# A hybrid encoder trunk: the passes for the attention row maxima in the projection stage, and two kinds of store on ScalarE's queue

## The chip, the cores and the metric

One core of one Trainium2 chip runs the whole program as one launch. The metric is the device time of that core in microseconds, the median over several executions. The profiles are each of one execution.

## The reference

Two batches of 1024 tokens (a "prompt" and a "sample") go through the same two layers. Each layer is a norm, one wide projection into four token mixers and their gates, the mixers, and one projection back:

```python
def _trunk(x, p):
    for l in range(DEPTH):
        h = _rmsnorm(x, p['norm_g'][l])
        zz = h @ p['w_in'][l]
        zA, zB, zC, zD = ...
        oA = _rwkv_mixer(zA, ...)          # A: matrix state, 4 heads of 64, both directions
        oB = _global_attn_mixer(zB, ...)   # B: 4 query heads on 2 key heads, rotary, all 1024 keys
        oC = _rglru_mixer(zC, ...)         # C: gated linear recurrence
        oD = _window_attn_mixer(zD, ...)   # D: window of 128 to both sides, ALiBi, a sink logit
        o = jnp.concatenate([oA, oB, oC, oD], -1) @ p['w_out'][l]
        x = x + o
    return _rmsnorm(x, p['final_g'])
```

B and D are softmax attention: `p = exp(s - m)`, with `m` the maximum of a query's row of scores (in D also of the sink). Any `m` near the maximum gives the same quotient.

## The kernel before

A unit u is one batch in one layer: u = 0, 1 are the two batches in layer 0, u = 2, 3 in layer 1. The program is written in the order `F0 F1 B0 O0 F2 B1 O1 F3 B23 O23`: F is `front` (norm, projections, mixers A and C), B is `mixer_bd` (attention of both kinds), O is the projection back. A scheduler at build time then fixes the order of the instructions on every engine, and each engine runs its own list strictly in that order. So parts of the program overlap: the long serial mixer A of a unit (chunks of 64 tokens, many small products on quarters of TensorE's array) runs beside that unit's projections, and its rest beside whatever follows.

**Projections.** `proj` makes a block of 128 output columns for all 1024 tokens: weights come in two pieces on ScalarE's queue, ScalarE rounds them (`wh`), GpSimd forms the rest (`wl`), and TensorE does 48 products of 512 columns into two PSUM buffers `pj`. A unit has 17 blocks that go to DRAM as `zd` (`proj_store`: ScalarE copies PSUM to `m`, SyncE's queue stores it) and 8 gate blocks (`proj_gate`). `ropes` normalises and rotates queries and keys of B and writes them back to `zd`; it uses the three PSUM buffers `px` and the SBUF buffers `rp`.

**Attention.** A unit has four jobs (`JOBS`): two of kind D, two of kind B, each with two query heads r on one key head. `attn_prep` loads queries and keys from `zd`, each twice, into both halves of the 128 partitions, and splits them into a rounded part and a rest (`ka`, `kb`, `qa`, `qb`). `attn_max` computes the row maxima: for each of the 8 blocks of 128 queries a product of 128 rows by 512 keys (B: two halves of the keys; D: up to 384 keys, and a second product that adds the ALiBi bias), and a `tensor_reduce` on VectorE (L930 in B, L942 in D). `put_max` turns the maxima round on TensorE, negates them on ScalarE, loads them as a row, and copies this into row 64 of `qb`, so that the scores' second product subtracts them. `attn_main` then goes over blocks of 128 keys: scores of both heads into `px`, exponentials on ScalarE (L982), the products with the values (L99), and sums of the exponentials on VectorE and GpSimd in turn (L995). `mixer_bd` steps the maxima of the next job between the blocks of the running job; those of the first job come before its first block.

## Time and profile before

| | |
|---|---|
| median of 3 runs | 3402.02 us (3401.68 to 3405.71) |
| the profiled execution: its time, its span | 3410.22 us, 3408.1 us |
| TensorE busy | 3097.8 us (91%) |
| VectorE busy | 1909.3 us (56%) |
| ScalarE busy | 1280.9 us (38%) |
| GpSimd busy | 1157.5 us (34%) |

A product's end is modelled, so that products of a dense stream overlap in the records, and 91% does not mean that TensorE could take no more. What bounds a stage has to be read stage by stage.

### The profile page before, as it was taken

The page shows a single profiled execution, that of the slowest core. Times are in us where ns is not written, and L with a number is a line of the kernel's source. Part 1 is how long each engine was busy: PE and PEld are TensorE (multiplying, and loading weights), DVE is VectorE, ACT ScalarE, POOL GpSimd, SP SyncE. Part 2 cuts the span into 40 slices and gives each one's busy share as a digit, 9 for nine tenths or more (in the row PEclk, how much of TensorE's full clock was granted, in tenths as well). Part 3 has the DMA queues.
Part 4 walks back from the last instruction along what each step waited for, and adds up shares of the span by engine and source line. Part 5 has one row for each costly group of instructions (what it writes and reads, how often), then busy time and mean ns, then how long its engine had stood idle before and what let it go on. Part 6 is the DMA issues. An engine that isn't in the chain of part 4 may idle for free.

```text
span 3408.1 us, 68337 instructions
## 1 busy us (share of the span) xinstructions
PE 3097.8 (91%) x27826; PEld 2166.3 (64%) x27826; DVE 1909.3 (56%) x3849; ACT 1280.9 (38%) x2429; POOL 1157.5 (34%) x1008
## 2 busy tenths in 40 slices
PE   6999999999789798999978988989999889977997
PEld 5777767766445576776756546766776555543586
DVE  6245344154887627135667765335563687698523
ACT  5332223225544324224444433226323434464322
POOL 2234232232433233223332333332332333435443
PEclk8999999999789897999968997889999779988999
DMA  7333333233310434233331015333333221123453
GB/s 248 116 106 102 92 112 96 90 102 103 105 43 24 135 122 123 79 94 101 121 101 56 20 45 163 113 100 104 115 105 96 76 68 36 37 63 133 161 200 133
DMA packets 382276, 344.06 MB, mean 101 GB/s; under 512 B 125709, under 2 KB 264969, under 8 KB 381961
## 3 DMA queue, kind: packets, MB, share of 16 engines
q1 hardware_dynamic: 242568, 270.48, 24.8%
q10 hardware_dynamic: 139392, 69.22, 7.2%
q8 instruction: 218, 3.57, 0.4%
q14 instruction: 98, 0.79, 0.1%
HBM read 217.84 MB, written 121.63 MB: 100 GB/s over the span
## 4 chain that ended last, share of the span: by engine, by line
PE 62%; DVE 19%; DMA 8%; ACT 4%; issue 4%; SPq 1%; POOL 1%; ACTq 0%; POOLq 0%; DVEq 0%
PE pj L101 36%; PE pa L101 11%; PE px L101 7%; PE pj L99 4%; DMA tg<-og 2%; DVE bk L567 1%; PE ps L101 1%; DVE bk L569 1%; DVE mxb L930 1%; SPq L95 1%; DMA halo<-zd 1%; DVE ac L995 1%; DVE b L904 1%; DMA bk<-nd 1%; DMA nd<-nl 1%
## 5 line engine op out<-in xcount | busy, mean ns | idle before, releaser
L101 PE MATMUL pj<-h,wh 128*128 128x512 f32 x3200 | 1072.7, 413 | 29.8 <-ACT h L236 11.0
L101 PEld LDWEIGHTS pj<-h,wh 128*128 128x128 f32 x3200 | 598.7, 191 | 217.0 <-issue 37.6
L326 POOL TENSOR_TENSOR wl<-wr,wh 128x512 fp32r<-128x512 f32 x264 | 351.7, 1332 | 951.5 <-ACT wh L325 848.8
L101 PE MATMUL pj<-h,wl 128*128 128x512 f32 x1600 | 645.9, 407 | 0.7 <-POOL wl L326 0.7
L101 PE MATMUL px<-b,b 128*128 128x512 f32 (+6 forms) x1072 | 361.5, 430 | 29.7 <-DVE mxb L930 12.7
L995 POOL TENSOR_TENSOR ac<-e,ac 128x512 f32<-128x512 f32 (+3 forms) x192 | 228.1, 1195 | 471.8 <-ACT e L982 321.8
L101 PEld LDWEIGHTS pj<-h,wl 128*128 128x128 f32 x1600 | 305.2, 191 | 82.9 <-issue 14.5
L101 PE MATMUL pj<-oh,wh 128*128 128x512 f32 x1024 | 334.3, 405 | 13.6 <-ACT oh L236 10.7
L101 PEld LDWEIGHTS px<-b,b 128*128 128x128 f32 (+1 forms) x1072 | 198.1, 207 | 221.3 <-issue 134.0
L325 ACT CAST wh<-wr 128x512 fp32r<-128x512 f32 x264 | 163.4, 619 | 465.7 <-PE pj L101 460.2
L982 ACT ACTIVATE e<-px 128x512 f32<-128x512 f32 (+3 forms) x384 | 191.4, 516 | 252.5 <-PE px L101 247.0
L101 PEld LDWEIGHTS pj<-oh,wh 128*128 128x128 f32 x1024 | 192.1, 191 | 64.8 <-ACT oh L236 14.6
L99 PE MATMUL pj<-e,v 128*64 128x512 f32 (+3 forms) x768 | 194.3, 573 | 11.7 <-ACT e L982 10.9
L101 PE MATMUL pj<-oh,wl 128*128 128x512 f32 x512 | 202.3, 400 | 0.0
L101 PE MATMUL pa<-ar,bk 64*64 64x128 f32 (+2 forms) x2560 | 142.7, 303 | 42.7 <-ACT nl L520 24.6
L995 DVE TENSOR_TENSOR ac<-e,ac 128x512 f32<-128x512 f32 (+3 forms) x192 | 144.3, 755 | 57.9 <-ACT e L982 38.0
L101 PEld LDWEIGHTS pa<-ar,bk 64*64 64x64 f32 x2560 | 106.5, 148 | 86.2 <-issue 42.8
L930 DVE TENSOR_REDUCE mxb<-px 128x1 f32<-128x512 f32 x160 | 108.2, 682 | 30.6 <-PE px L101 30.1
L348 ACT ACTIVATE m<-pj 128x512 f32<-128x512 f32 x136 | 80.8, 594 | 116.3 <-PE pj L101 100.3
L1081 DVE TENSOR_TENSOR xo<-xo,pj 128x512 f32<-128x512 f32 x64 | 43.8, 685 | 125.3 <-PE pj L101 97.4
L911 POOL TENSOR_TENSOR b<-rw,b 64x512 fp32r<-64x512 f32 x64 | 90.6, 1425 | 66.8 <-ACT b L910 66.0
L101 PEld LDWEIGHTS pj<-oh,wl 128*128 128x128 f32 x512 | 98.3, 192 | 21.6 <-issue 1.4
(285 smaller groups left out, 5010.9 us busy)
## 6 DMA issues: line engine op xcount, KB each, us to landing
wr<-in_w_in_dram ACTq DMA_DIRECT2D x200, 256.0 KB
zd<-m SPq DMA_DIRECT2D x136, 256.0 KB
tg<-og SPq DMA_DIRECT2D x64, 512.0 KB
rw<-zd SPq DMA_DIRECT2D x192, 128.0 KB
og<-m SPq DMA_DIRECT2D x64, 256.0 KB
wr<-in_w_out_dram ACTq DMA_DIRECT2D x64, 256.0 KB
xo<-xd SPq DMA_DIRECT2D x64, 256.0 KB
halo<-zd SPq DMA_DIRECT2D x56, 256.5 KB
```

The source lines that it names most:

```text
L95: self.nc.sync.dma_start(out=out, in_=src)
L99: return self.nc.tensor.matmul(out=out, lhsT=lhsT, rhs=rhs, start=start, stop=stop, skip_group_check=True)
L101: self.nc.tensor.matmul(out=out, lhsT=lhsT, rhs=rhs, start=start, stop=stop)
L325: nc.scalar.copy(out=hi, in_=raw)
L326: nc.gpsimd.tensor_tensor(out=lo, in0=raw, in1=hi.bitcast(F32), op=ALU.subtract)
L348: self.nc.scalar.mul(out=m, in_=p, mul=scale)
L567: nc.vector.tensor_tensor(out=ww, in0=m[:, j, j + 1:16].unsqueeze(2).to_broadcast([128, k, j + 1]), in1=t[:, j:j + 1, 0:j + 1].to_broadcas ...
L911: (nc.gpsimd if PQ else nc.vector).tensor_tensor(out=c[0:64, s], in0=t[0:64], in1=a[0:64, s].bitcast(F32), op=ALU.subtract)
L930: nc.vector.tensor_reduce(out=mx[:, i, half:half + 1], in_=p, axis=AX.X, op=ALU.max)
L982: last = nc.scalar.activation(out=e[:, :n], in_=p[:, :n], func=AF.Exp)
L995: (nc.gpsimd if (x + r) % ADDM else nc.vector).tensor_tensor(out=acc[r][:, os], in0=es[r][:, :n], in1=acc[r][:, os], op=ALU.add)
L1081: nc.vector.tensor_tensor(out=xo, in0=xo, in1=p, op=ALU.add)
```

## The change

The row maxima leave the attention. A generator `attn_maxes` runs inside `front`: for each of the four jobs it loads the keys of the head once more into both halves of the partitions and the queries of both heads, rounds both on ScalarE (`mk`, `rp`), and multiplies rounded queries with rounded keys only, head 0 on partitions 0 to 63 and head 1 on 64 to 127, so that the two heads' products use different halves of TensorE's rows. The reductions on VectorE are as many and as large as before. The maxima are stored to a DRAM tensor `rows`, from which `attn_prep` loads them. Four steps of the generator are written after each block of B's projections (a step: one block of queries, both heads, and in B one half of the keys), five after each gate block, and what is left after the last gate. The blocks are now written in the order D, B, C, with a step of `ropes` after each block of B and C. The stores of projected blocks and of maxima are issued on ScalarE's queue. `rp` has three buffers instead of five.

```diff
-MAXF = 1
-MXP = 3
-MXD = 3
+MAXB, MAXD = 5, 4
-BUFS = {..., "rp": 5, "cs": 1, ...
+BUFS = {..., "rp": 3, "mk": 2, "cs": 1, ...
...
+    def store_a(self, out, src):
+        self.nc.scalar.dma_start(out=out, in_=src)
...
     def proj_store(self, pool, wsrc, c0, h, dst, first=False, scale=1.0):
         def cb(half, p):
             m = self.t(pool, "m2")
             self.nc.scalar.mul(out=m, in_=p, mul=scale)
-            self.load(dst[:, HT * half:HT * half + HT], m)
+            self.store_a(dst[:, HT * half:HT * half + HT], m)
...
-    def put_max(self, pool, mr, qb):
...
     def attn_prep(self, pool, J):
...
+                row = self.t(pool, "rw")[64:65]
+                self.load(row, J["rows"][r].rearrange("n q -> (n q)").unsqueeze(0)[:, s])
+                nc.scalar.copy(out=c[64:65, s], in_=row)
...
-    def attn_max(self, pool, J, L):
...
+    def attn_maxes(self, pool, zd, L, rows, es):
+        def high(tag, srcs):
+            t = self.t(pool, "rp")
+            for hs, src in srcs:
+                self.load(t[hs], src)
+            h = self.t(pool, tag).bitcast(F32R)
+            nc.scalar.copy(out=h, in_=t)
+            return h
+        for job, (z, g) in enumerate(JOBS):
+            hs = [slice(HT * half, HT * half + HT) for half in range(2)]
+            kh = [high("mk", [(q, zd[z + 2][64 * g:64 * g + 64, s]) for q in HS]) for s in hs]
...
+            for i in range(NT):
+                if i % 4 == 0:
+                    qh = high("rp", [(slice(0, 128), zd[z + g][:, hs[i // 4]])])
+                q = lambda r: qh[HS[r], 128 * (i % 4):128 * (i % 4) + 128]
+                if z == ZD:
...
+                    for r in range(2):
+                        self.mm(ps[r][:, :n], self.slope[2 * g + r], self.alibi[:, b0:b0 + n], start=False, skip=True)
+                    for r in range(2):
+                        nc.vector.tensor_reduce(out=mx[r][:, i:i + 1], in_=ps[r][:, :n], axis=AX.X, op=ALU.max)
+                    yield
+                else:
+                    for half in range(2):
+                        ps = [self.px() for _ in range(2)]
+                        for r in range(2):
+                            self.mm(ps[r], q(r), kh[half][HS[r]])
+                        for r in range(2):
+                            nc.vector.tensor_reduce(out=mx[r][:, i, half:half + 1], in_=ps[r], axis=AX.X, op=ALU.max)
+                        yield
...
+                self.store_a(rows[job, r], m)
...
     def mixer_bd(self, units):
...
-            for _ in self.attn_max(pool, jobs[0], jobs[0]["L"]):
-                pass
             for i in range(len(jobs)):
-                nxt, ahead = iter(()), 0
                 if i + 1 < len(jobs):
                     start(i + 1)
-                    nxt = self.attn_max(pool, jobs[i + 1], jobs[i + 1]["L"])
...
+                self.attn_main(pool, jobs[i])
...
     def front(u):
...
                 k.mixer_a(keep, zd, L, od[0:2])
-                for b in range(2):
-                    k.proj_store(pool, wi, C_OFF + 128 * b, h, zd[ZC + b])
-                for b in range(4):
-                    k.proj_store(pool, wi, B_OFF + 128 * b, h, zd[ZB + b])
-                rope = k.ropes(pool, zd, L)
+                maxes = k.attn_maxes(pool, zd, L, rows, es)
                 for b in range(4):
                     k.proj_store(pool, wi, D_OFF + 128 * b, h, zd[ZD + b], scale=0.125 if b < 2 else 1.0)
-                    next(rope, None)
+                rope = k.ropes(pool, zd, L)
+                for off, n, z in ((B_OFF, 4, ZB), (C_OFF, 2, ZC)):
+                    for b in range(n):
+                        k.proj_store(pool, wi, off + 128 * b, h, zd[z + b])
+                        next(rope, None)
+                        for _ in range(MAXD if z == ZB else 0):
+                            next(maxes, None)
                 k.mixer_c(zd, L, od[4:6])
             for i, off in ((2, B_OFF + 512), (6, D_OFF + 512), (4, C_OFF + 256), (0, A_OFF + 896)):
                 for b in range(2):
                     k.proj_gate(pool, wi, off + 128 * b, h, gd[i + b])
-                    next(rope, None)
+                    for _ in range(MAXB):
+                        next(maxes, None)
+            for _ in maxes:
+                pass
```

Three places of the instruction order that the scheduler made.

VectorE, where unit 0 ends: before, from the last gate (L359) on. `m`, `h` in L307 and L237 are the norm of unit 1, `kt` is mixer A.

```order
L359 SCALAR_TENSOR_TENSOR m_901_6282<-m_901_6282,pj_6220 128x512
L359 SCALAR_TENSOR_TENSOR m_902_6286<-m_902_6286,pj_6221 128x512
L647 TENSOR_TENSOR kt_378_2205<-kt_378_2205,pa_2668 128x512
L307 SCALAR_TENSOR_TENSOR m_910_6310<-m_910_6310,par_122,rp_6301 128x512
L647 TENSOR_TENSOR kt_380_2207<-kt_380_2207,pa_2669 128x512
L307 SCALAR_TENSOR_TENSOR m_913_6317<-m_913_6317,par_122,rp_6308 128x512
L307 SCALAR_TENSOR_TENSOR m_914_6322<-m_914_6322,par_122,rp_6301 128x512
L237 TENSOR_TENSOR h_6313<-m_910_6310,h_6312 128x512
```

VectorE after the change, some 30 instructions behind the last gate of unit 0. L953 is the reduction of B's maxima, L692 the addition in the 14 state steps of mixer A (L689 before).

```order
L953 TENSOR_REDUCE mx_983_6366<-px_6372 128x1
L953 TENSOR_REDUCE mx_984_6367<-px_6373 128x1
L692 TENSOR_TENSOR z_258_1258<-z_258_1258,ps_2836 128x128
L953 TENSOR_REDUCE mx_983_6366<-px_6378 128x1
L953 TENSOR_REDUCE mx_984_6367<-px_6379 128x1
L953 TENSOR_REDUCE mx_983_6366<-px_6384 128x1
L692 TENSOR_TENSOR z_258_1258<-z_258_1258,ps_2842 128x128
L953 TENSOR_REDUCE mx_984_6367<-px_6385 128x1
L953 TENSOR_REDUCE mx_983_6366<-px_6390 128x1
L953 TENSOR_REDUCE mx_984_6367<-px_6391 128x1
L692 TENSOR_TENSOR z_259_1259<-z_259_1259,ps_2848 128x128
L953 TENSOR_REDUCE mx_983_6366<-px_6466 128x1
```

Before, the norm of unit 1 follows the last gate at once. Now 54 of unit 0's reductions stand behind that gate, in threes between mixer A's instructions, and the first instruction of unit 1's norm comes after the last of them. On TensorE, too, the first projection of unit 1 comes after unit 0's last product for maxima. In the four units 54, 49, 52 and 49 reductions, 204 of 384, stand behind the last gate; in units 1, 2 and 3 attention or its preparation follows.

TensorE after the change, in unit 0's projections. `pa` is mixer A, `px<-mk,rp` the new product of scores, `px<-alibi` the bias, `pj` a projection; the stretch had only `pa` and `pj` before.

```order
L103 MATMUL pa_1832<-na_270_1309,nl_264_1271 64x128
L103 MATMUL pa_1833<-na_272_1311,nl_264_1271 64x128
L101 MATMUL px_5100<-mk_5078,rp_5089 128x384
L101 MATMUL px_5100<-alibi,slope_456 128x384
L101 MATMUL px_5107<-mk_5078,rp_5089 128x384
L101 MATMUL px_5108<-mk_5078,rp_5089 128x384
L101 MATMUL px_5107<-alibi,slope_455 128x384
L101 MATMUL px_5108<-alibi,slope_456 128x384
L103 MATMUL pj_5269<-h_307,wh_5302 128x512
L103 MATMUL pj_5269<-h_306,wl_5303 128x512
L103 MATMUL pj_5269<-h_320,wh_5302 128x512
```

With three buffers `px` the products come in threes: one head alone first, then a pair of both heads. Of 208 pairs 146 stand next to each other. The 180 reductions that stand ahead of the last gates have 212 products of scores (128 reductions of D, whose blocks 3 and 4 need two products each, and 52 of B) and 128 of bias, in 75 such runs.

SyncE's queue in unit 0's projections: before, `zd<-m` are the stores of projected blocks, `nd`, `halo` and `wa` loads and stores of mixer A.

```order
L95 DMA zd_89<-m_218_1092 128x512
L95 DMA zd_89<-m_219_1095 128x512
L95 DMA zd_89<-m_228_1160 128x512
L95 DMA zd_89<-m_229_1163 128x512
L95 DMA nd_1576<-nl_264_1271 128x8x64
L95 DMA zd_89<-m_641_4758 128x512
L95 DMA zd_89<-m_642_4761 128x512
L95 DMA zd_89<-m_651_4826 128x512
L95 DMA zd_89<-m_652_4829 128x512
L95 DMA halo_1512<-zd_89 128x513
L95 DMA wa_1510<-wa_1505 128x512
L95 DMA halo_1519<-zd_89 128x513
```

After, at the place of mixer A's first inverse (`nd`, `td`, `bk` are its round trips through DRAM; `rp<-zd` are loads of ropes and of the maxima).

```order
L93 DMA bd_1260<-tp_1238 128x512
L93 DMA td_1577<-bk_287_1396 128x256
L93 DMA bk_287_1396<-td_1577 128x16x16
L93 DMA rp_5038<-zd_89 128x512
L93 DMA rp_5075<-zd_89 64x512 x2
L93 DMA rp_5080<-zd_89 64x512 x2
L93 DMA rp_5087<-zd_89 128x512
L93 DMA zd_89<-rp_5038 128x512
L93 DMA rp_5193<-zd_89 128x512
L93 DMA rp_5230<-zd_89 128x512
L93 DMA zd_89<-rp_5193 128x512
```

No store of a projected block is left on this queue; the loads for the maxima stand there instead, 64-row loads for keys and 128-row loads for queries, six for a job.

## Rows read from the trace of the kernel before

**Rows 1.** The page's first line

```profile
span 3408.1 us, 68337 instructions
```

**Rows 2.** Windows by stage: projections of units 0 and 1, three attention stages

```profile
core 0: us, PE busy (x) PEld busy (x) DVE busy (x) ACT busy (x) POOL busy (x), PEclk, DMA share, GB/s
...
57.00:421.00 364.00, 356.89 (x3077) 272.36 (x3078) 151.70 (x360) 118.53 (x231) 110.22 (x107) 1.00 0.38 117
...
456.00:836.00 380.00, 368.10 (x3536) 277.99 (x3535) 152.10 (x347) 117.91 (x221) 107.72 (x91) 1.00 0.31 93
836.00:1158.00 322.00, 266.92 (x2612) 152.96 (x2612) 258.01 (x487) 152.89 (x304) 120.27 (x113) 0.85 0.24 71
...
1718.00:2058.00 340.00, 288.70 (x3046) 176.46 (x3035) 248.69 (x504) 140.50 (x301) 115.69 (x112) 0.83 0.22 63
...
2633.00:3191.00 558.00, 482.55 (x4589) 275.95 (x4581) 432.48 (x796) 261.48 (x516) 220.87 (x185) 0.88 0.22 66
```

**Rows 3.** Groups by line: the reductions of the row maxima

```profile
L930 DVE TENSOR_REDUCE mxb<-px 128x1 f32<-128x512 f32 x160 | 108.2, 682 | 30.6 <-PE px L101 30.1
...
L942 DVE TENSOR_REDUCE mxd<-px 128x1 f32<-128x384 f32 (+1 forms) x80 | 41.2, 525 | 15.5 <-PE px L101 15.4
```

**Rows 4.** Windows: two attention jobs of kind B, the later one without maxima

```profile
3087.00:3151.00 64.00, 50.46 (x175) 20.61 (x170) 58.16 (x79) 30.18 (x54) 34.52 (x23) 0.93 0.46 157
3151.00:3192.00 41.00, 40.06 (x137) 15.82 (x136) 19.94 (x24) 18.35 (x34) 19.95 (x14) 0.90 0.04 13
```

**Rows 5.** Timeline of TensorE in the last attention job

```profile
3177.16 1.21 PE L101 MATMUL px<-b,b 128*128 128x512 f32 x4
...
3179.31 1.21 PE L101 MATMUL px<-b,b 128*128 128x512 f32 x4
...
3181.46 1.21 PE L101 MATMUL px<-b,b 128*128 128x512 f32 x4
```

**Rows 6.** Windows: last gate of a unit to the first exponential

```profile
836.00:880.00 44.00, 25.38 (x229) 16.81 (x230) 38.86 (x66) 31.58 (x48) 20.75 (x13) 0.76 0.49 150
...
1718.00:1766.00 48.00, 29.89 (x193) 22.25 (x183) 39.42 (x95) 21.76 (x48) 20.20 (x21) 0.62 0.54 154
...
2633.00:2674.00 41.00, 29.38 (x469) 21.38 (x462) 33.68 (x88) 19.14 (x41) 15.40 (x14) 0.59 0.50 143
```

**Rows 7.** Windows of the mixer's 14 state steps (L689 alone)

```profile
444.00:487.00 43.00, 4.00 (x14) 0.92 0.27 87
...
2702.00:2735.00 33.00, 3.93 (x14) 0.84 0.23 73
```

**Rows 8.** Timeline of TensorE: 64-row products between projections

```profile
113.04 1.12 PE L101 MATMUL pa<-wa,up 64*128 64x512 f32 x2
114.09 0.73 PE L101 MATMUL pj<-h,wh 128*128 128x512 f32 x2
...
165.05 0.63 PE L101 MATMUL pj<-h,wh 128*128 128x512 f32 x2
165.52 0.40 PE L101 MATMUL pj<-h,wl 128*128 128x512 f32 x1
165.85 1.13 PE L101 MATMUL pa<-wa,up 64*128 64x512 f32 x4
166.91 0.50 PE L101 MATMUL pj<-h,wh 128*128 128x512 f32 x1
```

**Rows 9.** Who waited for the maxima of kind B (us, times)

```profile
  PEld px L101: 22.9, 24
  PE pj L101: 17.6, 13
```

**Rows 10.** The waits of SyncE's queue, and one of the mixer on its loads

```profile
SPq L95 <- ACT m L348: 593.2, 118, 15.1
...
SPq L95 <- ACT mt L864: 223.1, 17, 33.3
...
ACT bk L579 <- DMA bk<-td: 44.7, 14, 8.6
```

More of the change, by code (lines that the diff above doesn't have):

```diff
@@ L250, in x_first @@
         h = []
+        rows = self.t(hpool, "cs", (128, 2, HT)) if hpool else None
         for half in range(2):
@@ L258, in x_first @@
             self.rms_finish(ss, st[:, 4 * half:4 * half + 4])
-            rb = self.norm_rows(hpool, st, half, self.px) if hpool else None
+            rb = self.norm_rows(rows, st, half, self.px) if hpool else None
             for d in range(ND):
@@ L275, in x_first, with norm_rows @@
         return h
-    def norm_rows(self, pool, st, half, ps):
+    def norm_rows(self, rb, st, half, ps):
         pb = ps()
@@ L282, in norm_rows @@
             self.mm(pb[:, 128 * j:128 * j + 128], st[:, i:i + 1].to_broadcast([128, 128]), self.ident)
-        r = self.t(pool, "rp", (128, 516))[:, 0:HT]
-        self.nc.scalar.copy(out=r, in_=pb)
-        return r
+        self.nc.scalar.copy(out=rb[:, half], in_=pb)
+        return rb[:, half]
     def rms_finish(self, ss, st):
@@ L296, in norm @@
         nc = self.nc
-        rb = [self.norm_rows(pool, st, half, self.pj) for half in range(2)]
+        rb = self.t(pool, "cs", (128, 2, HT))
+        rb = [self.norm_rows(rb, st, half, self.pj) for half in range(2)]
         h = []
@@ L856, in diag @@
                                      in1=x.unsqueeze(2).to_broadcast([128, n, 128]), op=ALU.mult)
-    def put_max(self, pool, mr, qb):
-        nc = self.nc
-        p = (self.pj if PJ & 2 else self.px)((NT, 128))
-        nc.tensor.transpose(out=p, in_=mr.bitcast(F32), identity=self.ident)
-        m = self.t(self.smp, "mt", (NT, 128), bufs=1)
-        nc.scalar.mul(out=m, in_=p, mul=-1.0)
-        for half in range(2):
-            row = self.t(pool, "e")[64:65]
-            self.load(row, m[4 * half:4 * half + 4])
-            nc.scalar.copy(out=qb[64:65, HT * half:HT * half + HT], in_=row)
     def values(self, pool, src):
@@ L983, in attn_main @@
                     es.append(e)
-                    yield
                 for r in range(2):
@@ L1012, in mixer_bd @@
             jobs = []
-            for zd, L, od in units:
+            for zd, od, rows, es in units:
                 vals = {}
-                for z, g in JOBS:
+                for n, (z, g) in enumerate(JOBS):
                     jobs.append({"g": g, "q": zd[z + g], "k": zd[z + 2][64 * g:64 * g + 64], "alibi": z == ZD, "z": z,
-                                 "vals": vals, "vs": zd[z + 3], "L": L, "o": od[(6 if z == ZD else 2) + g]})
+                                 "vals": vals, "vs": zd[z + 3], "rows": rows[n], "es": es[g],
+                                 "o": od[(6 if z == ZD else 2) + g]})
             def start(i):
@@ L1027, in mixer_bd @@
             start(0)
-            for _ in self.attn_max(pool, jobs[0], jobs[0]["L"]):
-                pass
             for i in range(len(jobs)):
-                nxt, ahead = iter(()), 0
                 if i + 1 < len(jobs):
                     start(i + 1)
-                    nxt = self.attn_max(pool, jobs[i + 1], jobs[i + 1]["L"])
-                    ahead = (16 if jobs[i + 1]["alibi"] else 32) * MAXF / (20 if jobs[i]["alibi"] else 32)
-                due = 0
-                for _ in self.attn_main(pool, jobs[i]):
-                    due += ahead
-                    while due >= 1:
-                        next(nxt, None)
-                        due -= 1
-                for _ in nxt:
-                    pass
+                self.attn_main(pool, jobs[i])
     def space(self, st, name, pad=0):
@@ L1174, in front @@
         od, gd = [[og[d][:, i] for d in range(ND)] for i in range(2)]
-        zog.append((zd, od, og))
+        rows = k.t(k.drp, "mx", (len(JOBS), 2, NT, 128), bufs=2)
+        es = [[], []]
+        zog.append((zd, od, og, rows, es))
         wi = w["w_in"][l]
```

58 lines of the change are left out of this document (27 added, 31 removed).

## The prediction

> **What bounds the kernel now.** I read the page first, then the span cut into stages, then the places where a stage could be seen with and without the maxima. The stages follow each other almost without overlap except for mixer A, which runs beside all of them. The reader should see two kinds [rows 2]. In the projections (57 to 421 us, 456 to 836) TensorE is busy 357 of 364 and 368 of 380 us at a granted clock of 1.00, which is the level of 2.4 GHz, and VectorE only about 152 us. So there TensorE is the bound. In the three attention stages (322, 340 and 558 us, 1220 us together) VectorE is busy 258, 249 and 432 us, 939 us or 77%, and the granted clock is a mean of the two levels, 0.83 to 0.88: TensorE waits at times. The row maxima lie entirely in these stages: 256 reductions of kind B at 0.68 us and 128 of kind D at about 0.53 us [rows 3], 174 + 68 = 242 us, a quarter of VectorE's work there.
>
> What a maximum costs the attention can be read near the end, where mixer A is done. The last job but one of kind B runs with the 32 reductions of the last job between its blocks and takes 64 us; the last job has none beside it and takes 41 us [rows 4]. In the first VectorE is busy 58 of 64 us, in the second 20 of 41. In the second TensorE sets the pace: a block of keys starts every 2.15 us (3177.16, 3179.31, 3181.46) [rows 5].
>
> **The change part by part.** The sum is made against the profiled execution's span of 3408.1 us [rows 1] and its own time of 3410.2 us, which lies 8.2 us above the median of 3402.0.
>
> *Maxima out of the attention.* 64 - 41 = 23 us for 32 reductions is 0.72 us each, slightly more than the reduction itself. For 256 of kind B that gives 184 us; for 128 of kind D I take the bare 0.53 us, 68 us: **-252 us**. The other bound: beside mixer A VectorE is busy only 77%, and if only that share of the gain is real it is -194 us. I take the first, because the places with and without differ by nothing else as large.
>
> *The start of an attention stage.* From a unit's last gate to the first exponential 44, 48 and 41 us pass [rows 6], 133 us. In them the first job's 16 reductions, two heads' blocks of kind D, have to run alone, and then come the transposition, the load and the copy of the maxima. 16 x 0.53 = 8.5 us of each start are already counted. Of the remaining 107 us I take 25 us a start, **-75 us**: preparation can run beside what now precedes it, while the rest is mixer A's and C's work, which stays. Bounds: 0 and -107 us.
>
> *204 reductions behind the last gates.* The order shows them in threes, each three before one of mixer A's state steps where those run. Fourteen such steps take 43 us in one place and 33 us in another [rows 7], so 3.07 and 2.36 us a step, and three reductions and the addition are 3 x 0.68 + 0.28 = 2.32 us. So three reductions cost a step of 2.36 to 3.07 us, 0.79 to 1.02 each. I take 0.9: **+184 us**. The lower bound is the 0.72 of above, 147 us, the upper 1.02, 208 us. Nothing covers them: unit 1's norm is queued behind them on VectorE, and TensorE's first projection behind that; in the other units the attention is.
>
> *180 reductions beside projections.* VectorE has the room, but TensorE, the bound there, gets 212 products of scores and 128 of bias more. A projection's product of 512 columns goes by in 0.235 us (two start from 165.05 to 165.52) [rows 8]. At 352 columns a reduction of kind D needs 0.16 us for scores and 0.16 us for bias, one of kind B 0.235 us: 21 + 21 + 12 = 54 us if the heads do not overlap. They can: one 64-row product of 512 columns takes 1.05 us alone (113.04 to 114.09), and two on different halves of the rows take 1.06 us together (165.85 to 166.91) [rows 8]. If all pairs overlapped it would be 37 us; the order leaves 70% of the pairs next to each other, so 42 us. To enter the 64-row form costs 165.85 - 165.52 - 0.235 = 0.095 us [rows 8]; 75 runs make 7 us. Then TensorE waits for a free `px`: in the attention 256 reductions of kind B cost it 22.9 + 17.6 us of waits [rows 9], 0.16 us each, and for 180 that is 28 us. Together **+77 us**; bounds 37 us (all overlap, no waits) and 54 + 7 + 56 = 117 us (no overlap, twice the waits).
>
> The Trainium skill ("TensorEngine Tiling (Array Packing)", Key Properties) says that a change of tiling mode drains TensorE, which speaks against putting these runs between projections. The trace shows less: the last full product before the pair is recorded to 165.92, and the pair begins at 165.85, before it. By the rule each of the two changes of a run would cost the 0.165 us that a product outlasts its turn, 25 us in place of 7, and the time would come out 18 us later, inside the range below.
>
> *Queues and casts.* 136 stores of blocks and 32 of maxima pass from SyncE's queue to ScalarE's, and 64 more casts of about 0.6 us come to ScalarE. ScalarE is busy 118 us of 364 and 380 in the projections [rows 2], and this adds some 10 us of casts and 42 issues a unit; even at 0.5 us an issue it stays under half busy. I count nothing; if every issue held up an eviction of `pj` for 0.3 us it would be 50 us in all. On SyncE's queue the waits for projected blocks (593 us in total) and for maxima (223 us) go away [rows 10]. That is time in which the queue stood still, and loads behind it were late only if something wanted them; I count nothing here either and keep it as a rival. The new order of blocks D, B, C and the three `rp` buffers only shift work that is off TensorE's path; nothing.
>
> Sum: -252 - 75 + 184 + 77 = **-66 us**, so 3344 us for a profiled execution and **3336 us** as the median, 1.9% less.
>
> **The rivals.**
>
> 1. *Slower: the projections stall.* What was 0.16 us a reduction in the attention may be more beside projections, since VectorE runs mixer A, ropes and reductions in one strict order, and a run of three products needs all three `px` empty. If each of the 75 runs waits for three reductions, 2.04 us, the waits are 153 us instead of 28, and the sum is +59: 3461 us. It turns slower when a run waits more than 1.2 us. For it: TensorE has no slack there. Against it: the order puts some ten projections between runs, 2.4 us in which VectorE can empty two buffers.
>
> 2. *The reductions behind the gates eat it all.* If they come at 1.22 us each instead of 0.9, because unit 1's norm and the attention's preparation follow them one after another on VectorE, the sum is zero: about 3402 us. For it: VectorE's order has the whole norm behind them. Against it: in units 1 to 3 only preparation follows.
>
> 3. *More gain: SyncE's queue was the brake of mixer A.* ScalarE waits 44.7 us in total for one of the mixer's loads [rows 10], and the longest wait of the queue for maxima is 33.3 us, with the mixer's loads behind it. If those waits go and as much is saved on the mixer's other loads, some 90 us more are gained where mixer A runs beside attention: 3246 us.
>
> 4. *The packing changes nothing for TensorE*, because the pairs do not overlap in this form of product: 54 instead of 42 us, 12 us later. It stays inside the forecast.
>
> **How the numbers follow.** My forecast with rival 4 gets 0.52, rival 1 0.24, rival 2 0.11, rival 3 0.13. All the best bounds together (-252 - 107 + 147 + 37 = -175) would give 3227 us, all the worst (-194 + 0 + 208 + 117 = +131) 3533 us; neither is likely as a whole. The forecast's own range is 3270 to 3395 us. With rival 3 and the milder half of rival 1 the range that should hold the time 8 times in 10 is 3255 to 3440 us. A measurement of this kernel can tell about 0.2%, 7 us, from no change. Faster by more than that: nearly all of the forecast, rival 3 and a little of rival 2, 0.65. Within: 0.08. Slower: rival 1 and what is left of 2 and of the forecast, 0.27.
>
> **What the profile after would show.** Right: the attention stages of units 0 and 1 shrink from 322 and 340 us to some 200 to 240 us with TensorE the busiest and the clock nearer 1.00; between a unit's last gate and the next stage 50 to 90 us appear in which VectorE is nearly full of reductions and TensorE waits; each projection stage grows by 15 to 30 us. Wrong: a projection stage grows by more than 35 us with waits of `px` on the reductions (rival 1); the stretch behind a gate lasts over 100 us (rival 2); mixer A ends well before the last attention job and its waits on loads are halved (rival 3). The prediction is wrong, too, if attention keeps more than 280 us without its maxima, since then VectorE's time was not what it waited for.

## The result, and the profile after

The change makes the kernel slower: 3461.5 us (median of 4 runs) against 3403.9 us, 1.0148 times as long, 95% interval 1.0124 to 1.0173. A second comparison on another occasion gave 1.0145 (1.0117 to 1.0172). The prediction was 3336 us, faster, in a range that ends at 3440 us; it was wrong in sign.

The profiled execution took 3465.1 us. The page's first lines and its row of TensorE's granted clock:

```profile
span 3462.9 us, 68630 instructions
...
PE 3130.0 (90%) x27858; PEld 2195.0 (63%) x27858; DVE 1908.3 (55%) x3849; ACT 1312.5 (38%) x2493; POOL 1161.2 (34%) x1008
...
PEclk9999979999967889899997698899999958998998
```

The windows that answer to [rows 2]: projections of units 0 and 1, then the three stretches from a unit's last gate to the first product of the projection back (columns as there):

```profile
54.00:443.00 389.00, 376.15 (x3251) 287.79 (x3251) 174.61 (x416) 129.30 (x255) 111.17 (x107) 0.99 0.39 122
547.00:958.00 411.00, 393.33 (x3504) 292.51 (x3503) 179.20 (x406) 147.34 (x259) 113.06 (x97) 0.98 0.32 99
958.00:1264.00 306.00, 256.94 (x2651) 152.48 (x2651) 189.80 (x371) 123.09 (x259) 106.72 (x103) 0.77 0.22 65
1853.00:2167.00 314.00, 262.11 (x2810) 159.19 (x2804) 210.18 (x411) 129.48 (x273) 109.76 (x103) 0.78 0.23 64
2756.00:3247.00 491.00, 418.21 (x3793) 232.52 (x3791) 352.18 (x567) 250.28 (x482) 219.95 (x181) 0.84 0.25 76
```

The stretches from gate to projection back, 322, 340 and 558 us before, are still 306, 314 and 491 us, though VectorE's busy time in them has fallen by 68, 39 and 80 us. The granted clock fell too, from 0.85, 0.83 and 0.88. Their first 66, 70 and 53 us hold reductions that were moved here (below). The attention itself follows, with 240, 244 and 438 us:

```profile
1024.00:1264.00 240.00, 205.77 (x2053) 121.43 (x2047) 130.72 (x235) 106.81 (x223) 97.89 (x90) 0.83 0.21 64
1923.00:2167.00 244.00, 207.19 (x2512) 127.50 (x2512) 151.96 (x280) 112.97 (x236) 101.07 (x91) 0.84 0.22 66
2809.00:3247.00 438.00, 372.99 (x3271) 202.58 (x3271) 305.18 (x474) 242.12 (x462) 213.98 (x175) 0.86 0.26 79
```

Between units 0 and 1, where 35 us lay before, 104 us lie now (443 to 547); both figures include the first, sparse products of unit 1.

Where the time went is best seen in a table of places. Each number is the distance between starts of TensorE's products in the trace, in us: first to last product of a unit's projections, last gate to first product with the values, first to last product with the values, and so on. The columns are rounded one by one.

| kernel | four projection stages | unit 0's last gate to unit 1's first | last gates to values (3) | products with values (3) | values to projection back (3) | projection back (3) | rest | span |
|---|---|---|---|---|---|---|---|---|
| before | 1618 | 10 | 57+60+47 | 251+250+509 | 21+30+3 | 454 | 98 | 3408 |
| after | 1720 | 67 | 95+88+81 | 191+202+408 | 21+25+3 | 469 | 94 | 3463 |
| difference | +102 | +57 | +100 | -209 | -5 | +15 | -4 | +55 |

A second profile of the same changed kernel has 1728, 69, 264 and 791 us in the first four columns (1720, 67, 264 and 801 here). So a difference of 10 us in one column is no finding.

Behind the last gates the reductions of the global heads run. The four stretches from a last gate to the last reduction (two of them and the sum; the second fence counts L953 alone):

```profile
443.00:506.00 63.00, 55.43 (x641) 38.38 (x639) 52.70 (x123) 14.52 (x35) 6.27 (x5) 0.69 0.20 57
...
1853.00:1923.00 70.00, 54.92 (x298) 31.69 (x292) 58.21 (x132) 16.51 (x38) 8.70 (x12) 0.55 0.23 59
...
sum 251.00, PE 205.74 PEld 130.43 DVE 216.56 ACT 54.75 POOL 29.77; mean PE 51.44 PEld 32.61 DVE 54.14 ACT 13.69 POOL 7.44
```

```profile
443.00:506.00 63.00, 34.44 (x55) 0.69 0.20 57
...
1853.00:1923.00 70.00, 34.24 (x52) 0.55 0.23 59
...
sum 251.00, DVE 130.72; mean DVE 32.68
```

VectorE is busy 217 of 251 us there, and only 131 of them are the 205 reductions. The other 86 us are nearly all work of mixer A that stands in the same list between them. VectorE's costliest groups in the second stretch (958 to 1024) are these:

```profile
L953 DVE TENSOR_REDUCE mx<-px 128x1 f32<-128x512 f32 x49 | 31.7, 678 | 3.8 <-PE px L103 3.8
L572 DVE TENSOR_TENSOR bk<-bk,bk 128x15 f32<-128x15 f32 (+7 forms) x15 | 3.0, 202 | 0.2
L570 DVE TENSOR_TENSOR bk<-bk,bk 128x15 f32<-128x15 f32 (+7 forms) x15 | 3.0, 201 | 0.2
L475 DVE SCALAR_TENSOR_TENSOR tp<-tp,kk 128x512 f32<-128x512 f32 x2 | 2.4, 1216 | 0.0
L493 DVE TENSOR_TENSOR ar<-kk,tp 128x504 f32<-128x504 f32 x2 | 2.2, 1095 | 0.0
```

### The profile page after: what moved, and what is told of

Read it like the earlier page. It is cut to its first block, busy times and chain, and to the rows that moved or that the text cites. A ratio compares the mean times of both kernels' runs of the same rounds, so it can differ in the third digit from the quotient of the medians.

```text
span 3462.9 us, 68630 instructions
## 1 busy us (share of the span) xinstructions
PE 3130.0 (90%) x27858; PEld 2195.0 (63%) x27858; DVE 1908.3 (55%) x3849; ACT 1312.5 (38%) x2493; POOL 1161.2 (34%) x1008
## 4 chain that ended last, share of the span: by engine, by line
PE 49%; DVE 17%; DMA 10%; ACT 5%; issue 4%; POOL 2%; SPq 1%; ACTq 0%; DVEq 0%; POOLq 0%
PE pj L103 26%; PE pa L103 9%; PE px L103 7%; PE pj L101 4%; DMA tg<-og 2%; DVE mx L953 1%; DMA rp<-zd 1%; DVE ac L1014 1%; DVE bk L572 1%; SPq L93 1%; DMA halo<-zd 1%; PE px L101 1%; PE ps L103 1%; DVE bk L570 1%; DMA rw<-zd 1%
## 5 line engine op out<-in xcount | busy, mean ns | idle before, releaser
L103 PE MATMUL pj<-h,wl 128*128 128x512 f32 x1600 | 638.9, 403 | 0.0
L103 PE MATMUL px<-b,b 128*128 128x512 f32 (+3 forms) x832 | 262.5, 421 | 20.1 <-ACT e L1002 13.8
L103 PEld LDWEIGHTS px<-b,b 128*128 128x128 f32 x832 | 152.8, 211 | 184.9 <-issue 140.2
L1002 ACT ACTIVATE e<-px 128x512 f32<-128x512 f32 (+3 forms) x384 | 183.4, 516 | 170.4 <-PE px L103 163.8
L1014 DVE TENSOR_TENSOR ac<-e,ac 128x512 f32<-128x512 f32 (+3 forms) x192 | 166.6, 877 | 128.2 <-ACT e L1002 85.5
L953 DVE TENSOR_REDUCE mx<-px 128x1 f32<-128x512 f32 x256 | 164.0, 680 | 31.1 <-PE px L103 29.1
L103 PE MATMUL px<-mk,rp 64*128 64x512 f32 x256 | 118.2, 666 | 19.2 <-DVE mx L953 13.9
```

The source lines that it names most:

```text
L103: self.nc.tensor.matmul(out=out, lhsT=lhsT, rhs=rhs, start=start, stop=stop)
L953: nc.vector.tensor_reduce(out=mx[r][:, i, half:half + 1], in_=ps[r], axis=AX.X, op=ALU.max)
L1002: last = nc.scalar.activation(out=e[:, :n], in_=p[:, :n], func=AF.Exp)
L1014: (nc.gpsimd if (x + r) % ADDM else nc.vector).tensor_tensor(out=acc[r][:, os], in0=es[r][:, :n], in1=acc[r][:, os], op=ALU.add)
```

## The experiments

The ratios are to the kernel before, run beside each. All edits also change the order that the build gives the engines' lists. That alone moved the same work from 0.9992 to 1.0145 (below), so a difference of 1% or so from a single build need not be the edit's.

**What the maxima were worth.** The kernel before without products and reductions of the maxima (the part for the global heads; the windowed heads' is cut in the same way):

```diff
...
-                for i in range(NT):
-                    for half in range(2):
-                        p = self.pj() if (2 * i + half) % MXP == 0 else self.px()
-                        self.mm(p, qa[r][:, 128 * i:128 * i + 128], ka[:, 512 * half:512 * half + 512])
-                        nc.vector.tensor_reduce(out=mx[:, i, half:half + 1], in_=p, axis=AX.X, op=ALU.max)
-                        yield
+                nc.gpsimd.memset(mx, 0.0)
+                yield
...
```

> The kernel before with the products and reductions of the row maxima left out (the maxima are set to a constant and the exponentials are taken of a hundredth of the scores, so that they stay finite; all other work is kept). If VectorE's reductions are what the attention stages wait for, as the prediction has it, the 252 us and the 75 us of the starts go: 3404 - 327 = about 3080 us, or 3140 us with the smaller bound of 194 us. If the attention stages are paced by something else (the rounds of mixer A in the same instruction lists, the chain score, exponential, product), the maxima are worth little there: 3300 us or more.

Measured 0.9845 (0.9808 to 0.9883): 3352 us, 56 us less than the 3408 beside it, about as much as the order of the lists can make. The values' products shrank to 198, 205 and 424 us and the starts by 40 us, 223 us in all. But at one place, from the last values to the last projection back, 156 us pass where it was 3 (second row; columns as above):

```profile
2530.00:2952.00 422.00, 376.37 (x4115) 212.13 (x4113) 272.08 (x501) 204.84 (x445) 182.20 (x173) 0.89 0.17 48
2952.00:3108.00 156.00, 67.45 (x1150) 44.43 (x1146) 93.04 (x165) 58.99 (x85) 24.67 (x20) 0.69 0.33 106
```

The timeline of TensorE at the end of that stretch:

```profile
3076.39 1.97 PE L101 MATMUL ps<-ident,ar 64*64 64x64 f32 x32 [2.49 <-DVE ar L718]
3108.25 0.80 PE L101 MATMUL pj<-oh,wh 128*128 128x512 f32 x1 [29.88 <-ACT oh L236]
```

The attention is over at 2952 us, and mixer A (`ps`) ends at 3078 us, where the kernel before has it end at 3087. The projection back needs both. It needs mixer C, too, whose last step ends at 3078 us as well and stands on the chain that ended last. Without mixer A that step is over at 1842 us, before the last gate (the run without mixer A and maxima, below), so mixer C is late behind mixer A.

The same two kernels without mixer A:

```diff
-                k.mixer_a(keep, zd, L, od[0:2])
+                az = k.t(keep, "az", (128, T), bufs=1)
+                k.nc.gpsimd.memset(az, 0.0)
+                for i in range(2):
+                    k.load(od[i], az)
```

> The kernel before with mixer A left out (its two blocks of the output are stored as zeros). Theory of the reductions: VectorE's maxima pace the attention stages, which keep 230 us or more each without mixer A, since the reductions stay. Theory of mixer A: its rounds in the same lists are what TensorE waits for, and the attention stages of units 0 and 1 fall from 250 us (first to last product of the values) to 170 us or less.

> The kernel before without mixer A and without the products and reductions of the maxima (constants in their place, exponentials of a hundredth of the scores). The kernel before without mixer A took 2610 us. If mixer A keeps what the maxima would give back, leaving them out gives more here than the 52 us with mixer A: 150 us or more, 2460 us or less. If the attention stages do not wait for the reductions, it gives 60 us or less: 2550 us or more.

Measured 2609.9 us (0.7649) and 2467.1 us (0.7228): without mixer A, leaving all maxima out gives 143 us, nearly three times the 56 with it, though a little under the 150 expected. So mixer A, with mixer C behind it, did keep most of the gain in the experiment above. The reductions did not pace the attention alone either: without mixer A the values' products of units 0 and 1 fell from 251 and 250 to 160 and 156 us, as the theory of mixer A had it. The values' stretch of unit 0, both times without mixer A, first with the maxima and then without:

```profile
727.00:887.00 160.00, 145.19 (x579) 70.74 (x578) 106.08 (x167) 69.26 (x140) 67.70 (x60) 0.92 0.09 30
```

```profile
723.00:847.00 124.00, 114.66 (x484) 53.55 (x485) 62.66 (x88) 67.68 (x139) 72.81 (x66) 0.95 0.13 43
```

36 us for the 78 of the unit's 96 reductions that start in this stretch are 0.46 us each. Over the whole kernel it is 143 us for 384, 0.37 us each.

The opposite, each reduction issued twice in the kernel before:

> The kernel before with each of the 384 reductions of the maxima issued twice (0.53 to 0.72 us each by the rows of before, 250 us of VectorE's time more). Left out, they gave back 52 us of a 327 us that the prediction saw in them. If the attention stages do not wait for the reductions, doubling costs little as well: 3404 to 3500 us. If they do, and the gain of leaving them out is kept by mixer A, doubling costs nearly its whole 250 us: 3600 us or more.

Measured 1.0366 (1.0333 to 1.0399), 122 us: between the two expectations, so neither holds; it is half of what the added reductions take on VectorE.

**The change without mixer A.**

> The changed kernel with mixer A left out in the same way. Both theories look at its distance to the kernel before without mixer A. If mixer A took the place of the maxima as what the attention stages wait for, the change gains without it: 60 us or more faster than the kernel before without mixer A, and the products of the values of units 0 and 1 span 140 us or less. If the change costs time for other reasons (the passes in the projections and behind the gates), it stays slower without mixer A too, by 30 us or more.

Measured 2723.6 us (0.7984): 114 us slower than 2609.9. The theory that mixer A alone takes the place of the maxima falls, though its sign in the values came: 124 us in units 0 and 1. By the table's places: values -35, -32, -83; last gates to values +49, +47, +48; unit 0 to unit 1 +54; the four projection stages +67. Here all 64 reductions of a unit's global heads stand behind the last gate, and the stretch is about as long as with mixer A (some 60 us each, their sum below): 16 to 18 us until the first, then one every 0.67 to 0.70 us.

```profile
sum 243.00, PE 167.70 PEld 77.33 DVE 167.04 ACT 29.72 POOL 25.49; mean PE 41.93 PEld 19.33 DVE 41.76 ACT 7.43 POOL 6.37
```

**The passes left out of the changed kernel.**

> The changed kernel with the loads, products and reductions of the passes left out (maxima constant, exponentials of a hundredth of the scores; rows are still stored and loaded). Its distance to the changed kernel is what the passes cost in the projection stage and behind the gates: 184 + 77 = 261 us by the prediction's sum, so 3200 us. Its distance to the kernel before without its maxima is what all the rest of the change costs (queues, rows through memory, order): nothing by the prediction, more than 20 us if a queue or the order of the lists is to blame.

Measured 1.0731 (1.0699 to 1.0764), 3655 us where 3200 were expected, slower than with the passes. The build put SyncE's loads for attention behind those of mixer A, and the values begin 482, 270 and 272 us after the last gates; they then take 125, 123 and 282 us with nothing beside them. So the run can't price the passes; it shows what an order of the lists can cost.

**Queues, or the order of the lists.** Both stores back on SyncE's queue, the projections' stores alone moved in the kernel before, and each store alone in the changed kernel (the first of these edits):

```diff
     def store_a(self, out, src):
-        self.nc.scalar.dma_start(out=out, in_=src)
+        self.nc.sync.dma_start(out=out, in_=src)
```

> The changed kernel with both kinds of store put back on SyncE's queue, the passes left where the change put them. If the queues cost nothing, as the prediction's sum has it, the time stays within 10 us of the changed kernel's 3461 us. If the stores on ScalarE's queue are what made the change slower, it falls to 3410 or less. If they bring the gain that rival 3 gives them (66 us), it rises to about 3520 us.

> The kernel before with one part of the change alone: its stores of projections are issued on ScalarE's queue. By the prediction's sum no change (within 7 us of 3404). If the move helps by freeing SyncE's queue, 3340 us (rival 3's 66 us); if the issue on ScalarE holds up what stands behind it there, 3420 us or more.

> The changed kernel with only the rows of maxima back on SyncE's queue, so that the stores of projections alone are issued on ScalarE's. Both stores back gave 1.0004 times the kernel before, neither back 1.0145. If it is the stores of projections (136 of them, behind the copies of the passes in ScalarE's list, which wait for their loads) that cost time beside the passes, this run stays at 1.012 or more. If it is the rows, it comes to 1.003 or less. If only the order of the lists makes the difference, it lies anywhere, and neither half explains the whole.

> The changed kernel with only the stores of projections back on SyncE's queue, so that the rows of maxima alone are issued on ScalarE's. If the stores of projections are what cost time, this run comes to 1.003 times the kernel before or less; if the rows are, it stays at 1.012 or more.

Measured 1.0004 (0.9982 to 1.0027), 0.9980 (0.9960 to 1.0001), 1.0087 (1.0054 to 1.0120) and 1.0019 (0.9998 to 1.0040). The third lies between its expectations. Taken alone this would say that ScalarE's queue costs 50 us beside the passes. The control does the same work on the same queues in other lists:

```diff
-MAXB, MAXD = 5, 4
+MAXB, MAXD = 4, 3
```

> The changed kernel with the passes handed out three at a time beside the global heads' projections and four at a time behind the gates (4 and 5 before): the same work on the same queues, in other compiled lists. If ScalarE's queue is what costs 50 us, this stays at 1.012 or more of the kernel before; if the order of the lists is, it may come out as low as 1.003.

> The same with both stores on SyncE's queue. If ScalarE's queue is what costs, this stays at 1.003 or less of the kernel before; if the order of the lists is, the distance between this run and the one on ScalarE's queue comes out other than 50 us, of either sign.

Measured 0.9992 (0.9975 to 1.0010) on ScalarE's queue and 1.0027 (1.0006 to 1.0049) on SyncE's. The distance turned its sign, so no cost of the queue is shown; what differs is the order. In the first of them the four stretches behind the gates take 220 us instead of 251:

```profile
sum 220.00, PE 183.97 PEld 110.14 DVE 193.19 ACT 50.15 POOL 29.54; mean PE 45.99 PEld 27.53 DVE 48.30 ACT 12.54 POOL 7.39
```

**Is it TensorE, or its clock?**

```diff
+                    if not alibi:
+                        self.mm(p[:, :n], ka[:, ks], qa[r][:, qs], stop=False, skip=True)
                     self.mm(p[:, :n], ka[:, ks], qa[r][:, qs], stop=False)
```

> The changed kernel as it is, beside the others on the same chip: 1.0 to 1.7 per cent above the kernel before, as in its first comparison (1.0148).

> The changed kernel with the first product of each key block of the global attention issued twice into the same place (256 products more, about 0.22 us each at full clock, 56 us in all). Theory of the clock: TensorE is granted less than full clock in the attention stages because too little is issued there; with more products the granted clock of these stages rises from 0.82 to 0.86 to 0.90 or more and the time does not rise, or falls by up to 40 us. Rival: the clock is only a sign of the waiting; then the products cost what they take, 40 us or more.

Measured 1.0145 for the changed kernel and 1.0134 (1.0108 to 1.0160) with 256 products more: 3459.0 against 3461.5 us. The values' stretches of the changed kernel, then with the products:

```profile
1052.00:1243.00 191.00, 176.96 (x1609) 98.80 (x1607) 106.57 (x190) 85.47 (x183) 78.92 (x72) 0.84 0.14 39
1940.00:2143.00 203.00, 182.06 (x1888) 106.78 (x1890) 130.13 (x244) 94.68 (x197) 88.81 (x79) 0.88 0.16 47
2837.00:3244.00 407.00, 353.41 (x3110) 189.09 (x3108) 286.81 (x433) 220.62 (x421) 198.57 (x164) 0.88 0.25 75
```

```profile
1053.00:1249.00 196.00, 185.37 (x1673) 105.83 (x1673) 103.66 (x190) 88.48 (x183) 77.68 (x74) 0.89 0.13 39
1942.00:2132.00 190.00, 179.20 (x1912) 105.33 (x1914) 124.39 (x241) 92.70 (x189) 88.19 (x79) 0.96 0.16 45
2805.00:3228.00 423.00, 382.48 (x3372) 216.66 (x3370) 280.12 (x447) 230.53 (x432) 205.61 (x167) 0.90 0.25 74
```

The time stays and the clock is higher, as the theory of the clock had it; the rival, 40 us or more, did not come. But part of the rise is not the products' doing. The second profile of the changed kernel without them shows 0.83, 0.93 and 0.87 in its three stretches, 791 us long together; the middle one:

```profile
1942.00:2133.00 191.00, 172.20 (x1886) 101.11 (x1884) 129.18 (x243) 94.03 (x196) 88.77 (x79) 0.93 0.17 49
```

The stretches with the products take 809 us, 8 and 18 us more than in the two profiles without. This run can't tell whether the products filled waits or the higher clock paid for them. Nor does it show them free to within some tens of us, since its lists are other ones. That the clock is only a sign of the waiting is not shown.

**Why the global heads' passes come late.** The rotary steps end late in the changed kernel. The last instruction of each of unit 0's six steps (count, duration in ns, first and last start in us, form) before, after, and with the passes off their ring; the last gates end at 420, 443 and 438 us:

```profile
L841 POOL TENSOR_TENSOR rp<-rp,rp x6: 1287/1300/1481, 247.9 to 352.5; 128x512 f32<-128x512 f32 x6
```

```profile
L844 POOL TENSOR_TENSOR rp<-rp,rp x6: 1259/1289/1295, 234.3 to 416.1; 128x512 f32<-128x512 f32 x6
```

```profile
L844 POOL TENSOR_TENSOR rp<-rp,rp x6: 1276/1289/1296, 232.3 to 388.1; 128x512 f32<-128x512 f32 x6
```

```diff
...
-            t = self.t(pool, "rp")
+            t = self.t(pool, tag)
...
-            h = self.t(pool, tag).bitcast(F32R)
+            h = t.bitcast(F32R)
...
-                    qh = high("rp", [(slice(0, 128), zd[z + g][:, hs[i // 4]])])
+                    qh = high("mq", [(slice(0, 128), zd[z + g][:, hs[i // 4]])])
```

> The changed kernel with the passes off the ring that the rotary steps use: keys and queries are loaded into buffers of their own and rounded in place; the ring of three is the rotary steps' alone; the buffers for projections fall from four to three. Theory: the global heads' passes wait for the rotary steps, which end 27 to 38 us before the last gate since they share the ring (61 to 77 us in the kernel before). Then they end 50 us or more before it, the four stretches behind the gates (253 us in all) shorten to 200 us or less, and the time falls to 1.000 of the kernel before or below. Rival: the passes themselves are what doesn't fit beside the gates; then the stretches stay at 240 us or more and the time within 10 us of the changed kernel (1.0145).

Measured 1.0091 (1.0061 to 1.0120). The steps end 50, 45, 48 and 50 us before the last gates, and 174 reductions instead of 205 stand behind these; yet the four stretches take 257 us (their sum):

```profile
sum 257.00, PE 200.59 PEld 132.56 DVE 205.30 ACT 63.14 POOL 33.42; mean PE 50.15 PEld 33.14 DVE 51.32 ACT 15.79 POOL 8.36
```

The ring explains how many reductions come late, not how long the stretch is: my theory of it falls. Of the half per cent that came back much lies in the values' stretches (753 us for 801, or 791 in the second profile), so it isn't the ring's alone.

**Half of the change.** Only the windowed heads' maxima move, the global heads' stay in the attention stage:

```diff
...
-        for job, (z, g) in enumerate(JOBS):
+        for job, (z, g) in enumerate(JOBS[:2]):
...
```

> Half of the change, both stores on SyncE's queue: only the maxima of the windowed heads (128 reductions, which lie beside the projections before the last gate) are moved to the projection stage, those of the global heads (256 reductions, which stood behind the last gates in the changed kernel) stay in the attention stage as before. Theory: what the change loses is the stretch behind the gates, where the global heads' reductions run (253 us in the four stages), and what it gains there is the start of the attention stages and the windowed heads' share. Then this half is faster than both kernels: the starts gain 75 us, the products of the values 40 to 70 us, the projections lose 50 to 70 us: 3320 to 3370 us where the kernel before has 3404. Rival: the passes cost in the projections what they save, whichever they are: 3400 us or more.

> The same half of the change with both stores on ScalarE's queue. If these stores cost time wherever passes stand in the projection stage, it is 30 to 50 us slower than the half on SyncE's queue; if they cost only together with the global heads' passes behind the gates, the two agree within 10 us.

> Only the windowed heads' maxima in the projection stage, stores on ScalarE's queue (0.9944 of the kernel before), with the passes off the rotary steps' ring. Theory: the ring holds up the rotary steps and with them the projections; then the projections, 9 to 27 us longer each than in the kernel before, lose less and the time falls below 0.990. Rival: the projections lose what the passes' products take on TensorE, ring or not: 0.992 to 0.997.

Measured 1.0024 (1.0003 to 1.0045), 0.9944 (0.9922 to 0.9967) and 1.0068 (1.0046 to 1.0091). The second, 3393 us where the kernel before had 3409, beats both kernels, though not by what was expected (3320 to 3370 us). Its places against before: starts -65 (75 expected), values -78 (40 to 70), projections +66 (50 to 70); but from the last values to the projection back, with mixer A ending at 3121 us, 38 us pass instead of 3, and the projection back takes 25 us more. The other two are the same half, one on the other queue and one off the ring, in other lists, and both are a little slower than the kernel before; so what is shown is one good order of the half, not that the half gains in every order. The ring's theory falls here too: the third lies outside both its expectations, and off the ring the projections lose 98 us, not less.

## Why the prediction was wrong

The sum was -66 us; the span grew by 55 us. By its own terms:

| step | predicted | measured in the trace |
|---|---|---|
| maxima out of the attention (values) | -252 | -209 |
| start of the attention stages | -75 | -90 (164 us from gates to values before; 264 after, less 190 of the stretches of reductions) |
| reductions behind the last gates | +184 | +253 (last gate to last reduction 63, 68, 70, 52) |
| passes beside projections | +77 | +102 |
| queues and casts | 0 | no sign of its own (below) |
| projection back and around it; unit 0 to unit 1 without its stretch | 0 | +6; -6 |

**The step that failed most is "204 reductions behind the last gates".** The count was right (205), the price of 0.9 us was not: it was 1.23 us each, and the 253 us lie outside the upper bound of 208. The price took mixer A's state steps for all that stands between the reductions. In the trace the first and the fourth stretch hold 14 of these steps each, the second and the third none; all four hold other work of mixer A, most of the 86 us, and VectorE is busy 217 of 251 us. It is rival 2's price (1.22) by another cause: not unit 1's norm or the preparation, of which there is next to nothing in these stretches, but mixer A in the same list. That is read off the list; no run shows how long the stretches would be with the same 205 reductions and nothing else. Without mixer A they take 243 us, but with 256 reductions and a late start; off the ring 257 us with 174. The loss may come back partly in the first term, since what mixer A does here it no longer does beside the attention.

**"The places with and without differ by nothing else as large" was false.** The 64 us job of [rows 4] held more than maxima. VectorE's groups in that window:

```profile
L1066 DVE SCALAR_TENSOR_TENSOR tg<-tg 128x512 f32<-128x512 f32 x16 | 14.3, 894 | 2.6 <-DMA tg<-og 2.4
...
L930 DVE TENSOR_REDUCE mxb<-px 128x1 f32<-128x512 f32 x19 | 12.7, 679 | 0.7 <-PE px L101 0.7
L237 DVE TENSOR_TENSOR oh<-tg,oh 128x512 fp32r<-128x512 f32 x8 | 9.1, 1141 | 0.0
L930 DVE TENSOR_REDUCE mxb<-pj 128x1 f32<-128x512 f32 x11 | 7.5, 677 | 0.0
```

L1066 and L237 prepare the last projection back: 23.4 us, as much as the whole difference of 23 us from which 0.72 us a reduction was taken. Without mixer A a reduction was worth 0.46 us in the stretch shown. The term came out at -209 us, near its other bound (-194); with the maxima left out and put nowhere else the same places lost 182 us.

**"180 reductions beside projections" was too cheap,** +102 and not +77, inside its bounds. Rival 1 gave 3461 us, the very time measured, but by luck, since its cause is not there: between 250 and 380 us, where reductions run beside projections, TensorE's products have waited for another engine at this one place (us, times, longest), and none for `px`:

```profile
PE pj L103 <- DVE m L362: 5.5, 2, 2.8
```

In all four projection stages the waits that end with a reduction come to 4 us, weight loads included, so the 28 us that the sum had for them were not there either. What was missed stands in the changed kernel without mixer A, where only the windowed heads' 128 reductions lie beside projections and these grow by 67 us, 0.52 us each. TensorE's timeline of such a run:

```profile
304.75 1.03 PE L103 MATMUL pj<-h,wh 128*128 128x512 f32 x2
305.72 0.44 PE L101 MATMUL px<-mk,rp 64*128 64x384 f32 x1
306.09 0.44 PE L101 MATMUL px<-alibi,slope 128*128 128x384 f32 x1
306.46 0.44 PE L101 MATMUL px<-mk,rp 64*128 64x384 f32 x2
306.83 0.61 PE L101 MATMUL px<-alibi,slope 128*128 128x384 f32 x2
```

A 64-row product of scores and the 128-row product of the bias start 0.37 us apart, where 384 columns at 0.235 us for 512 [rows 8] take 0.18. The sum counted a change of row form once per run (75 times 0.095 us); there is one at every bias as well, 166 in the four stages of the changed kernel. From each start to the next product's start the passes' products hold TensorE there for 78 us, where the sum had 49; where the other 24 of the 102 us go is not shown. The weight loads of that run show one thing more: in the stream of projections a load begins ahead of its product (307.11 for the product at 307.29), at a change only with it (306.09).

```profile
306.09 0.19 PEld L101 LDWEIGHTS px<-alibi,slope 128*128 128x128 f32 x1 [0.19 <-issue]
...
307.11 0.19 PEld L103 LDWEIGHTS pj<-h,wl 128*128 128x128 f32 x1
```

The rule of the Trainium skill ("TensorEngine Tiling (Array Packing)", Key Properties) that a change of mode drains TensorE, which the prediction set aside, fits these 0.37 us; no run here tells the drain from the late load. Rival 4 does not hold: at 306.46 the products of both heads go by in the time of one.

**Queues at nothing** is not contradicted, but the order of the lists hides what a queue may cost: of three pairs that differ in the queue, one lost 1.4% on ScalarE's and two gained 0.35% and 0.8%.

**The signs.** The prediction set the stretches behind the gates apart (50 to 90 us, VectorE nearly full), and they came at 52 to 70. What is left of the attention, 240 and 244 us, is the edge of the 200 to 240 it named; its sign against itself, over 280, did not come unless those stretches are counted in (306 and 314). The clock is 0.83 and 0.84, not nearer 1.00. Unit 1's projections grew by 47 us, more than the 35 named for rival 1, without its waits. Rival 3 did not happen: mixer A ends at 3160 us, later than before.

Behind all terms lies one that the sum did not have: how much could be won. Without any maxima, and with none to be paid elsewhere, the kernel before gains 56 us with mixer A and 143 us without it. Against the cost that the prediction itself saw, 261 us, neither makes the change pay, unless most of that cost falls where the kernel waits anyhow. All seven builds of the whole change lie between 0.9992 and 1.0148, so the 1.9% forecast came in none; that this one loses 1.5% is one order's share. What stays open is why one order of the same work gives 0.9992 and another 1.0145: the stretches behind the gates account for 31 us of the 62 between the two traces (3401 and 3463 us), the rest is spread over the stages.

## What to carry to other kernels

Before moving work off a stage, leave it out altogether and time that: here it was 56 us, a sixth of the 327 us that the prediction had for it, because the serial work of mixers A and C ended behind it. When work is put into a stretch, price the stretch by everything in that engine's list, not by the moved instructions. And where a scheduler orders the lists, build the same work in a second order before blaming an edit for 1%.

## What the runs showed of the hardware

With 256 more products of 512 columns the changed kernel took the same time (1.0134 for 1.0145), and the granted clock of the three attention stretches was 0.89, 0.96 and 0.90, where two profiles without them have 0.84 and 0.83, 0.88 and 0.93, 0.88 and 0.87. Behind the gates TensorE is recorded as busy for 55 of 70 us and is granted 0.55 (1853 to 1923 us), so most of it is spent at the lower of its two levels (1.2 GHz); a busy share in the trace is no sign that the clock is full. And alternating 64-row with 128-row products of 384 columns cost about 0.19 us a change (0.37 us from start to start for 0.18), as long as a weight load, which there began only with its product.
